# The conditioning of a two-layer diffusion trunk, from row sums on VectorE to matmuls in column groups of TensorE

## The chip, the core and the metric

The kernel runs on one core of a Trainium2 chip. Four engines compute: TensorE (PE in the profile; PEld is its weight loading), VectorE (DVE), ScalarE (ACT) and GpSimd (POOL). SyncE (SP) issues the transfers. Each engine works through its own instructions in order and waits on semaphores for the others. The metric is the device time of one execution in microseconds.

## What is computed

Two layers of a trunk work on 512 latent tokens and 128 context tokens, 1024 wide. Every sub-layer norms its input, scales and shifts it by a conditioning vector, mixes, norms again, multiplies by a gate and adds the residual. The conditioning is one small product for each layer: two vectors of 1024 (one for latent tokens, one for context tokens) times a matrix of 1024 x 6144, cut in six pieces of 1024.

```python
silu_c = jax.nn.silu(c); silu_ctx = jax.nn.silu(c_ctx)
for l in range(DEPTH):                      # 2 layers
    mp = split_mod(silu_ctx @ w_mod[l] + b_mod[l])          # six pieces of 1024
    ms = split_mod((silu_c @ w_mod[l] + b_mod[l])[:, None, :])
    g = norm_g[l]
    hp = modulate(xp, g[0], mp[0], mp[1])   # rmsnorm(x, g) * (1 + scale) + shift
    hs = modulate(xs, g[0], ms[0], ms[1])
    ...                                     # mixer: attention and convolution, or pooling and Fourier
    xp = gated_residual(xp, yp, g[1], mp[2])                # x + gate * rmsnorm(y, g)
    xs = gated_residual(xs, ys, g[1], ms[2])
    hp = modulate(xp, g[2], mp[3], mp[4]); hs = modulate(xs, g[2], ms[3], ms[4])
    xp = gated_residual(xp, swiglu(hp, ...), g[3], mp[5])
    xs = gated_residual(xs, swiglu(hs, ...), g[3], ms[5])
```

So there are 12 pieces, (layer, i) with i from 0 to 5: i = 0 and 3 are shifts, 1 and 4 scales, 2 and 5 gates. Each piece reads 4 MB of weights.

## The kernel before

All large products are made of three matmuls of rounded operands (helper `mm3`, lines 230 to 232: high x high, high x low, low x high), so a weight tile is cast on ACT (L195, L694) and its rest is subtracted on DVE or POOL (L196, L630). The stages follow each other: the opening (norm of the input, transposes, modulation, the first head's Q, K and V), attention and the convolution units, the output projection (`project`, L510) with the chain of norm, gate and residual for each of five token tiles (`chain`), the feed-forward layer in Strassen's form (`ffn`, `strassen`) and its down projection (`project` again), then the same with the odd mixer. In the stages with a written order (`manual_schedule`) DVE, ACT and PE issue in the order in which the code emits; helpers such as `after(d, f)` and `tick` place small steps between matmuls by an estimated clock.

**Conditioning in the opening.** Pieces (0,0) and (0,1) are needed first. Half of each comes as columns of the product: `mod_mm` (L991) is a matmul with two stationary columns (the two vectors) and 256 moving columns of weights, four for a transfer of 512 KB. The other half comes as row sums on DVE: `dot` (L1018) multiplies a 128 x 1024 tile of transposed weights by a broadcast row and sums, once for each vector. A few products of the second vector go to POOL (`dot_pool`) with the sum on ACT. The string START gives the order of all that, engine by engine.

**The other ten pieces** come as such row sums in later stages: `mod_steps` loads eight tiles of 128 x 1024 for a piece and issues two row sums for each (L315); where `MP` says so the second vector's product is on POOL (L305) and its sum on ACT (L308). The generators are advanced one step at a time: (0,2), (0,4), (0,3) in attention and the convolution units (`steps`; what is left is emitted after the last unit), `M0` in Strassen's part of the feed-forward layer 0, `M1` in its down projection, `M2` in the odd mixer, `M4` in the last down projection. A piece ends with small DVE steps (`mod_finish`), and a gate also with a transpose and a store to DRAM (`mod_gate`), from where `gate_rows` (L354) loads it broadcast into the two buffers `t_g`. In attention those two buffers hold the broadcast rows of the row sums until the last of them is done.

Of the kernel before, what the change touches and what calls it, by code (L numbers as in the profile page):

```python
# [19 lines left out]
D = 1024  # L20
# [25 lines left out]
def plan_of(n_cl):  # L46
# [43 lines left out]
).split()  # L90
START_DVE = [5, 7]
# [11 lines left out]
AE = [2.5, 2.8, 4, 5.2]  # L103
DUP = 6
ADD = [5.3]
AC = [0.7, 1, 1.7, 3.4, 4.6]
M0 = [(0,5),(1,0)]
M1 = [(1,1),(1,2)]
M2 = [(1,4),(1,3)]
M3 = []  # L110
M5 = []
M4 = [(1,5)]
DT = [0,1]
# [8 lines left out]
ODD = 'm0 m0 V0 L2 F2 m0 m0 m0 D0 m0 P3 m0 m0 m0 V1 m0 L6 F6 m0 m0 P2 m0 m0 D1 L1 F1 m0 m0 m0 m0 V2 L7 m0 m0 F7 m0 m0 m0 P1 m0 L0 m0 m0 D2 F0 V3 m0 m0 D3 P0 m0 m0 m0 m0 m0 m0'.split()  # L122
DSL = ([1, 3, 6, 10, 12],[])
# [5 lines left out]
def trunk_kernel(ctx: ExitStack, tc: tile.TileContext, a: dict, o: dict):  # L129
# [53 lines left out]
    subg = const.tile([128, 128], F32)  # L183
    junk_a = const.tile([128, D], BF16)
    junk = {}
    mcol = const.tile([128, 2, 6, 2, 8], F32)
    acol = const.tile([128, 2, 2, 2, 8], F32)
    bcol = const.tile([128, 2, 2, 2, 8], F32)
    grow = dr.tile([2, 2, 16, 128], F32)
    srow = dr.tile([2, D], F32)  # L190
    xd = dr.tile([5, 128, D], F32)

# [71 lines left out]
    def mod_finish(l, i):  # L264
        for v in range(2):
            m = mcol[:, l, i, v]
            s = i // 3
            dve.tensor_tensor(out=m, in0=m, in1=bmod[:, l, i], op=ALU.add)
            if i % 3 == 0:
                dve.tensor_copy(bcol[:, l, s, v], m)  # L270
            elif i % 3 == 1:
                dve.scalar_tensor_tensor(out=acol[:, l, s, v], in0=m, scalar=1.0, in1=ng[:, l, 2 * s],
                                         op0=ALU.add, op1=ALU.mult)
            else:
                dve.tensor_tensor(out=m, in0=m, in1=ng[:, l, 2 * s + 1], op=ALU.mult)

    def mod_gate(l, i):
        if i % 3 == 2:
            s = i // 3
            while not free["tr"]:  # L280
                e = pending.pop(0)
                clock[0] = max(clock[0], e[0])
                e[2]()
            tp = trb()
            pe.transpose(tp[:16, :128], mcol[:, l, i].rearrange("p v k -> p (v k)"), ident)
            gs = junk[1]
            act.activation(out=gs, in_=tp[:16, :128], func=AF.Copy)
            nc.sync.dma_start(out=grow[l, s], in_=gs)

    def mod_steps(l, i, rows, get, share=(), early=lambda: True):  # L290
# [1608 lines left out]
```

## Time and profile before

| | before |
|---|---|
| three runs, us | 1460.73, 1461.1, 1469.1 (median 1461.1) |
| profiled execution, its span | 1460.5 us |
| PE busy | 1358.6 us, 93% of the span |
| PEld busy | 1241.1 us, 85% |
| DVE busy | 1143.7 us, 78% |
| ACT, POOL busy | 670.8 us (46%), 208.5 us (14%) |
| mean granted TensorE clock | 0.978 of 2.4 GHz |
| chain that ended last | PE 58%, DVE 26%, issue 6%, ACT 4%, DMA 4% |
| read from memory | 192 MB, 137 GB/s over the span |

The profiled execution's span is 0.6 us under the median of the runs. Busy time is summed over an engine's instructions; the idle time of an engine matters only where that engine is the one that the others wait for. A mean over the span hides that the stages have different limits, so the stretches below are read one by one.

### The profile page before, as it was taken

Reading aid. Unit: us, or ns where it says so; the run is one execution under the profiler, and the core shown is the slowest. Engines: PE = TensorE matmul, PEld = TensorE weight load, DVE = VectorE, ACT = ScalarE, POOL = GpSimd, SP = SyncE. Lnnn points to the kernel's source line nnn. Section 1 sums busy time; section 2 is a strip of 40 time slices with the busy share of each in tenths; the row PEclk is TensorE's granted clock in tenths of the full one; section 3 lists DMA queues with packets and bytes.
Section 4 is the critical chain, followed back from the end, with each engine's and each line's share of the span. In section 5 each row is a group of like instructions: output and inputs, shape, how many; then the busy total and the mean of one; then the engine's idle time right before and its main releaser. Section 6 shows DMA issues by size and latency. Waiting matters only on the chain.

```text
span 1460.5 us, 20973 instructions
## 1 busy us (share of the span) xinstructions
PE 1358.6 (93%) x7892; PEld 1241.1 (85%) x7892; DVE 1143.7 (78%) x2120; ACT 670.8 (46%) x1298; POOL 208.5 (14%) x109
## 2 busy tenths in 40 slices
PE   8898898978889999999998998898899999999997
PEld 3787788977789999999886788777899999997886
DVE  6767876598989978986989589858977777769475
ACT  6445554333555454544336542335454545443343
POOL 2321101342650000000004022006400000000000
PEclk9899999979989999999999999999999999999999
DMA  9412212265433324326763444623122222266452
GB/s 362 149 48 78 79 46 88 89 219 196 142 106 131 116 87 160 130 88 238 259 209 132 156 164 146 222 93 139 61 87 87 88 87 88 87 231 217 144 209 80
DMA packets 61070, 202.06 MB, mean 138 GB/s; under 512 B 9316, under 2 KB 11300, under 8 KB 60968
## 3 DMA queue, kind: packets, MB, share of 16 engines
q1 hardware_dynamic: 60968, 200.71, 39.1%
q8 instruction: 62, 1.02, 0.3%
q14 instruction: 40, 0.33, 0.1%
HBM read 192.26 MB, written 8.43 MB: 137 GB/s over the span
## 4 chain that ended last, share of the span: by engine, by line
PE 58%; DVE 26%; issue 6%; ACT 4%; DMA 4%; POOL 0%; SPq 0%; DVEq 0%; ACTq 0%
PE t_acc L510 13%; PE t_acc L230 10%; PE t_acc L231 10%; PE t_acc L232 10%; DVE t_sm L243 4%; DVE t_pg L315 4%; PE t_tr L230 4%; PE t_tr L232 4%; PE t_tr L231 4%; DVE t_lo L196 2%; PE t_tr L510 2%; DVE t_x L379 1%; DVE t_pg L375 1%; DMA t_pg<-in_w_mod_dram 1%; DVE t_lo L315 1%
## 5 line engine op out<-in xcount | busy, mean ns | idle before, releaser
L230 PE MATMUL t_acc<-t_q,t_hi 128*128 128x320 f32 (+2 forms) x680 | 218.0, 321 | 5.3 <-DVE t_q L1224 2.1
L232 PE MATMUL t_acc<-t_q,t_lo 128*128 128x320 f32 (+2 forms) x696 | 218.7, 314 | 0.2 <-POOL t_lo L196 0.2
L231 PE MATMUL t_acc<-t_q,t_hi 128*128 128x320 f32 (+2 forms) x680 | 214.2, 315 | 3.1 <-POOL t_q L435 3.1
L510 PE MATMUL t_acc<-t_hi,t_pg 128*128 128x512 f32 x696 | 192.0, 391 | 5.5 <-DVE t_pg L196 4.6
L195 ACT ACTIVATE t_hi<-t_raw 128x1024 fp32r<-128x1024 f32 (+1 forms) x110 | 113.5, 1033 | 144.6 <-PE t_acc L510 61.6
L196 POOL TENSOR_TENSOR t_lo<-t_raw,t_hi 128x1024 fp32r<-128x1024 f32 (+1 forms) x36 | 84.0, 2344 | 609.3 <-DVE t_sm L243 407.0
L510 PEld LDWEIGHTS t_acc<-t_hi,t_pg 128*128 128x128 f32 x696 | 129.6, 188 | 35.4 <-DVE t_pg L196 7.3
L230 PEld LDWEIGHTS t_acc<-t_q,t_hi 128*128 128x128 f32 x680 | 131.7, 194 | 6.8 <-ACT t_x L1235 2.4
L231 PEld LDWEIGHTS t_acc<-t_q,t_hi 128*128 128x128 f32 x680 | 131.6, 194 | 3.8 <-POOL t_q L435 3.6
L232 PEld LDWEIGHTS t_acc<-t_q,t_lo 128*128 128x128 f32 x696 | 134.4, 193 | 0.5 <-POOL t_lo L196 0.5
L196 DVE TENSOR_TENSOR t_lo<-t_raw,t_hi 128x1024 fp32r<-128x1024 f32 (+1 forms) x74 | 92.5, 1249 | 46.7 <-ACT t_hi L195 46.4
L510 PE MATMUL t_acc<-t_hi,t_q 128*128 128x512 f32 x416 | 118.4, 402 | 5.5 <-DVE t_pg L1472 2.9
L694 ACT ACTIVATE t_hi<-t_raw 128x512 fp32r<-128x512 f32 x140 | 87.4, 624 | 78.2 <-DVE t_raw L630 78.2
L630 DVE TENSOR_TENSOR t_raw<-t_raw 128x512 f32<-128x512 f32 x160 | 112.0, 720 | 2.2
L630 DVE TENSOR_TENSOR t_lo<-t_raw,t_lo 128x512 fp32r<-128x512 f32 x140 | 97.2, 695 | 21.0 <-ACT t_lo L694 20.7
L630 DVE TENSOR_TENSOR t_hi<-t_raw,t_hi 128x512 fp32r<-128x512 f32 x140 | 96.2, 698 | 14.4 <-ACT t_hi L694 14.4
L510 PE MATMUL t_acc<-t_lo,t_pg 128*128 128x512 f32 x348 | 107.2, 389 | 0.0
L315 DVE SCALAR_TENSOR_TENSOR t_pg<-t_pg,t_g 128x1024 bf16<-128x1024 f32 x80 | 97.6, 1219 | 7.2 <-DMA t_pg<-in_w_mod_dram 6.4
L510 PEld LDWEIGHTS t_acc<-t_hi,t_q 128*128 128x128 f32 x416 | 79.7, 194 | 23.1 <-issue 3.3
L694 ACT ACTIVATE t_lo<-t_raw 128x512 fp32r<-128x512 f32 x140 | 86.8, 620 | 0.6 <-DVE t_raw L630 0.6
L510 PEld LDWEIGHTS t_acc<-t_lo,t_pg 128*128 128x128 f32 x348 | 65.3, 188 | 13.7
L230 PE MATMUL t_acc<-t_q,t_lo 128*128 128x320 f32 x248 | 76.7, 309 | 0.0
(317 smaller groups left out, 3307.5 us busy)
## 6 DMA issues: line engine op xcount, KB each, us to landing
t_raw<-in_w_down_dram SPq DMA_DIRECT2D x56, 512.0 KB, 3.9
t_raw<-in_w_gate_dram SPq DMA_DIRECT2D x44, 512.0 KB, 4.2
t_raw<-in_w_up_dram SPq DMA_DIRECT2D x44, 512.0 KB, 4.2
t_pg<-in_w_mod_dram SPq DMA_DIRECT2D x40, 512.0 KB, 5.4
t_pg<-in_w_down_dram SPq DMA_DIRECT2D x26, 512.0 KB, 5.1
t_x<-in_w_mod_dram SPq DMA_DIRECT2D x24, 512.0 KB, 3.9
t_q<-in_w_mod_dram SPq DMA_DIRECT2D x16, 512.0 KB, 9.0
t_raw<-in_w_mod_dram SPq DMA_DIRECT2D x16, 512.0 KB, 3.9
```

Source lines behind the costliest of these rows:

```text
L195: act.activation(out=hi, in_=src, func=AF.Copy)
L196: (lo_eng or dve).tensor_tensor(out=lo, in0=src, in1=hi.bitcast(F32), op=ALU.subtract)
L230: pe.matmul(out, lhsT=l[0], rhs=r[0], start=start, stop=False, skip_group_check=more)
L231: pe.matmul(out, lhsT=l[0], rhs=r[1], start=False, stop=False, skip_group_check=more)
L232: pe.matmul(out, lhsT=l[1], rhs=r[0], start=False, stop=stop, skip_group_check=more)
L243: return lambda: dve.scalar_tensor_tensor(out=out, in0=in0, scalar=scalar, in1=in1, op0=op0, op1=ALU.mult)
L315: dve.scalar_tensor_tensor(out=junk[0], in0=raws[ft], scalar=1.0, in1=rows[v], op0=ALU.mult, op1=ALU.mult, accum_out=dst)
L375: dve.tensor_tensor(out=P["y"][:, b * 512:(b + 1) * 512], in0=ps[:, b], in1=g[:, b * 512:(b + 1) * 512], op=ALU.mult)
L379: eng.scalar_tensor_tensor(out=x, in0=P["y"], scalar=rs1, in1=x, op0=ALU.mult, op1=ALU.add)
L510: pe.matmul(ps[t][b] if t in parted else ps[t][:, b], lhsT=L[i][:, cols], rhs=w[j][:, b * 512:(b + 1) * 512], start=first and i + j == 0, ...
L630: eng.tensor_tensor(out=out, in0=in0, in1=in1, op=op)
L694: act.activation(out=t_op[:, 0], in_=A[key], func=AF.Copy)
```

## The change

All conditioning is done as fp32 matmuls on TensorE. `col_groups` issues four matmuls for one tile of 128 input rows: each has 32 stationary columns (two of them are the two vectors for this tile, the other 30 are further columns of the same buffer, whose results nobody reads), takes its own 256 (in the opening 128) moving columns of weights, and is placed in its own quarter of the array's columns and of the output's partitions. A piece is eight such groups, summed in PSUM or, in attention, added up by DVE (`gather`); then a copy, two transposes and `mod_finish`. The row sums on DVE, the products on POOL, the sums on ACT and the broadcast rows are gone. The weights of the ten later pieces are no longer transposed on the host.

```diff
+    def col_groups(out, k, rhs, start, stop):
+        n = out.shape[-1]
+        for j in range(4):
+            pe.matmul(out[32 * j:32 * j + 32], lhsT=csil[:, 2 * k:2 * k + 32], rhs=rhs(j), start=start, stop=stop,
+                      tile_position=(0, 32 * j))
+        spend(4 * n)
...
-                dve.scalar_tensor_tensor(out=junk[0], in0=raws[ft], scalar=1.0, in1=rows[v], op0=ALU.mult,
-                                         op1=ALU.mult, accum_out=dst)
+        load(max(ahead(), 1))
+        P = trb()[:, :256] if hold else None
+        for k in range(8):
+            load(k + 1)
+            if not hold:
+                P = tr_when_free()[:, :256]
+                free["tr"] -= 1
+            raw = raws[k]
+            col_groups(P, k, lambda j: raw[:, j * 256:(j + 1) * 256], k == 0 or not hold, k == 7 or not hold)
+            load(k + 1 + ahead())
+            if not hold:
+                def gather(P=P, k=k):
+                    if k:
+                        dve.tensor_tensor(out=R, in0=P, in1=R, op=ALU.add)
+                    else:
+                        dve.tensor_copy(R, P)
+                    free["tr"] += 1
+                after(0.4, gather)
+            yield
+        if hold:
+            R = get()[:, :256]
+            act.activation(out=R, in_=P, func=AF.Copy)
+            yield
...
+        tp = tr_when_free()
+        for h in range(2):
+            pe.transpose(tp[:, h * 128:(h + 1) * 128], R[:, h * 128:(h + 1) * 128], ident)
+        mod_finish(l, i, tp[:, :256])
...
-M0 = [(0,5),(1,0)]
-M1 = [(1,1),(1,2)]
+M0 = [(0,5),(1,0),(1,1)]
+M1 = [(1,2)]
...
     def mods():
         for i in (2, 4, 3):
-            yield from mod_steps(0, i, rows, lambda: xslot([128, D]), MP, lambda: wide)
+            yield from mod_steps(0, i, lambda: xslot([128, D]), amisc[:, :256], lambda: len(wide))
...
-    def mod_mm(e, q, i, half):
+    def mod_mm(e, q, half):
+        if half == 0:
+            vec[q, "o"] = trb()[:, :128]
+        w = pieces[q, half].rearrange("p (k i f n) -> p k i f n", k=2, i=2, f=2)
+        for k in range(2):
+            col_groups(vec[q, "o"], 2 * half + k, lambda j: w[:, k, j // 2, j % 2], half + k == 0, half + k == 4)
...
-    "T.T1 L.r41 D.sl0 T.mm110 A.Tc1 L.q111 A.m1 D.d05 T.F0 L.w3 A.h1 P.l1 L.w2 D.co5 D.d14 T.mm111 A.m5 "
+    "T.T7 D.Tc7 A.sp0 P.sl0 A.h0 D.l0 D.m1 A.h1 P.l1 L.q22 L.q23 T.mm10 T.mm11 T.F0 T.mm12 T.mm13 A.ro1 A.sp1 "
```

The opening is now four stages q of two feature tiles each: four transfers of 512 KB for a stage, four calls of `mod_mm`, a copy (`ro`), a transpose (`ct`), the coefficients on DVE (`cd`), then modulation (`m`), high part (`h`), low part (`l`) and the Q, K, V matmuls of the two feature tiles (`F`).

PE in the opening, from its first instruction. Before (L953 broadcasts the vectors, L991 is `mod_mm`, L977 transposes the input, L1001 the coefficients, L230 is the first of Q, K, V):

```order
L953 MATMUL t_tr<-t_raw,t_q 128x512 x4
L991 MATMUL t_tr<-t_q,csil 2x256 x8
L977 MATMUL t_acc<-ident,t_x 128x128 x30
L991 MATMUL t_tr<-t_q,csil 2x256 x8
L977 MATMUL t_acc<-ident,t_x 128x128 x5
L1001 MATMUL t_tr<-ident,t_pg 128x2 x4
L991 MATMUL t_tr<-t_q,csil 2x256 x8
L977 MATMUL t_acc<-ident,t_x 128x128 x5
L991 MATMUL t_tr<-t_q,csil 2x256 x4
L230 MATMUL t_acc<-t_hi,t_q 128x384
```

And now (L261 is `col_groups`, L948 the transposes, L970 a stage's coefficients, L222 the first of Q, K, V):

```order
L948 MATMUL t_acc<-ident,t_x 128x128 x15
L261 MATMUL t_tr<-t_q,csil 32x128 x8
L948 MATMUL t_acc<-ident,t_x 128x128 x5
...
L970 MATMUL t_tr<-ident,t_q 128x128
L948 MATMUL t_acc<-ident,t_x 128x128 x5
L261 MATMUL t_tr<-t_q,csil 32x128 x16
L222 MATMUL t_acc<-t_hi,t_q 128x384
```

The broadcasts are gone, and the 32 matmuls of 256 columns have become 128 of 128 columns, eight for each of 16 transfers. The last 16 stand behind the Q, K, V matmuls of the sixth feature tile, and the seventh and eighth behind them.

PE in Strassen's part of the feed-forward layer 0, at the border of two products. Before:

```order
L230 MATMUL t_acc<-t_q,t_hi 128x320
L231 MATMUL t_acc<-t_q,t_hi 128x320
L232 MATMUL t_acc<-t_q,t_hi 128x320
L230 MATMUL t_tr<-t_x,t_lo 128x320
L231 MATMUL t_tr<-t_x,t_lo 128x320
L232 MATMUL t_tr<-t_x,t_lo 128x320
```

And now:

```order
L222 MATMUL t_acc<-t_q,t_hi 128x320
L223 MATMUL t_acc<-t_q,t_hi 128x320
L224 MATMUL t_acc<-t_q,t_hi 128x320
L261 MATMUL t_tr<-t_g,csil 32x256 x4
L222 MATMUL t_tr<-t_x,t_lo 128x320
L223 MATMUL t_tr<-t_x,t_lo 128x320
L224 MATMUL t_tr<-t_x,t_lo 128x320
```

A group of four stands between the products here, and at 23 further such borders of this stage.

DVE at the end of the convolution units and the start of the output projection. Before (L315 is a row sum, L196 the low part of a weight tile, L268 `mod_finish`, L370 the start of the first chain):

```order
L315 SCALAR_TENSOR_TENSOR t_pg,mcol<-t_x,t_g 128x1024 x2
L1464 SCALAR_TENSOR_TENSOR t_pg<-t_pg,cw 128x642 x2
L268 TENSOR_TENSOR mcol<-mcol,bmod 128x8
L272 SCALAR_TENSOR_TENSOR acol<-mcol,ng 128x8
...
L315 SCALAR_TENSOR_TENSOR t_pg,mcol<-t_x,t_g 128x1024 x2
L196 TENSOR_TENSOR t_lo<-t_pg,t_hi 128x1024
L315 SCALAR_TENSOR_TENSOR t_pg,mcol<-t_x,t_g 128x1024 x2
L268 TENSOR_TENSOR mcol<-mcol,bmod 128x8
L270 COPY bcol<-mcol 128x8
```

And now (L319 is `gather`, L1404 a convolution step, L271 `mod_finish`, L188 a low part):

```order
L188 TENSOR_TENSOR t_lo<-t_raw,t_hi 128x1024
L319 TENSOR_TENSOR t_g<-t_tr,t_g 128x256 x3
L1390 MEMSET t_pg 128x1
...
L271 TENSOR_TENSOR mcol<-t_tr,bmod 128x8 x2
L274 COPY bcol<-mcol 128x8 x2
L1404 SCALAR_TENSOR_TENSOR t_pg<-t_pg,cw 128x642 x2
L188 TENSOR_TENSOR t_lo<-t_pg,t_hi 128x1024
```

The long row sums between the low parts are gone, the last piece, (0,3), is finished ahead of the last steps of the convolution units and no longer behind low parts of the output projection's weights, and what DVE still does for a tile of conditioning weights there is one addition of 128 x 256.

## Rows read from the trace of the kernel before

**Rows 1.** Stretches: from:to, length, busy of each engine, PE clock, DMA share, GB/s.
```profile
0.00:66.00 66.00, 54.79 (x240) 35.75 (x240) 45.78 (x82) 36.42 (x58) 18.84 (x13) 0.95 0.71 259
66.00:281.00 215.00, 191.54 (x1256) 182.23 (x1257) 145.93 (x327) 108.43 (x288) 34.45 (x16) 0.98 0.22 72
281.00:360.00 79.00, 67.77 (x339) 59.51 (x338) 72.99 (x119) 28.40 (x44) 29.79 (x11) 0.89 0.59 206
360.00:440.00 80.00, 67.12 (x373) 61.05 (x372) 72.78 (x140) 43.31 (x77) 44.49 (x26) 0.91 0.35 119
440.00:680.00 240.00, 240.00 (x1636) 239.73 (x1636) 214.63 (x383) 117.32 (x235) 0.00 (x0) 1.00 0.35 126
680.00:760.00 80.00, 78.77 (x347) 64.59 (x346) 71.00 (x114) 27.91 (x41) 0.00 (x0) 1.00 0.76 262
...
880.00:940.00 60.00, 53.58 (x314) 49.23 (x312) 57.44 (x107) 16.52 (x34) 10.20 (x4) 0.97 0.50 169
...
1300.00:1461.00 161.00, 150.73 (x666) 124.11 (x664) 102.34 (x178) 61.28 (x93) 0.00 (x0) 0.99 0.50 175
```
**Rows 2.** Row sums by line: duration ns min/median/max, first and last start.
```profile
L315 DVE SCALAR_TENSOR_TENSOR t_pg<-t_pg,t_g x80: 1210/1218/1227, 438.4 to 1344.8; 128x1024 bf16<-128x1024 f32 x80
...
L315 DVE SCALAR_TENSOR_TENSOR t_pg<-t_x,t_g x24: 1206/1219/3418, 279.8 to 348.9; 128x1024 bf16<-128x1024 f32 x24
...
L315 DVE SCALAR_TENSOR_TENSOR t_lo<-t_raw,t_hi x16: 1207/1220/3248, 865.6 to 935.4; 128x1024 bf16<-128x1024 f32 x16
...
L315 DVE SCALAR_TENSOR_TENSOR t_q<-t_x,t_g x12: 1215/1219/2848, 82.6 to 196.4; 128x1024 bf16<-128x1024 f32 x12
```
**Rows 3.** Timeline, PE, opening: start us, us, line, operation, count.
```profile
21.80 3.62 PE L991 MATMUL t_tr<-t_q,csil 128*2 128x256 f32 x16
```
**Rows 4.** Timeline, PE, attention: four transposes between the matmuls of a product.
```profile
71.65 0.60 PE L1247 MATMUL t_tr<-ident,t_q 128*128 128x128 f32 x4
72.01 0.39 PE L230 MATMUL t_acc<-t_q,t_hi 128*128 128x320 f32 x1
72.24 0.30 PE L231 MATMUL t_acc<-t_q,t_hi 128*128 128x320 f32 x1
72.38 0.31 PE L232 MATMUL t_acc<-t_q,t_lo 128*128 128x320 f32 x1
```
**Rows 5.** Stretches of the opening, columns as in rows 1.
```profile
0.00:10.00 10.00, 5.82 (x6) 1.66 (x6) 1.47 (x9) 4.64 (x8) 0.20 (x4) 1.00 0.71 256
10.00:20.00 10.00, 8.94 (x33) 3.80 (x34) 6.45 (x16) 7.35 (x13) 1.83 (x1) 1.00 1.03 412
20.00:30.00 10.00, 10.00 (x59) 5.01 (x57) 9.79 (x15) 5.77 (x10) 3.66 (x2) 1.00 1.01 403
```
**Rows 6.** Timeline, opening: coefficient copy, modulation, low part; last of Q, K, V.
```profile
25.45 0.59 ACT L996 ACTIVATE t_pg<-t_tr 2x512 f32<-2x512 f32 x1 [1.59 <-PE t_tr L991]
25.84 0.80 DVE L1047 TENSOR_SCALAR t_pg<-t_pg,acol,bcol 128x512 f32<-128x512 f32 x2
...
31.32 0.82 DVE L1056 TENSOR_TENSOR t_q<-t_pg,t_q 128x640 fp32r<-128x640 f32 x1
...
51.23 0.33 PE L231 MATMUL t_acc<-t_lo,t_q 128*128 128x384 f32 x1
51.40 0.34 PE L232 MATMUL t_acc<-t_hi,t_q 128*128 128x384 f32 x1
...
65.44 0.34 PE L232 MATMUL t_acc<-t_hi,t_q 128*128 128x384 f32 x1
```
**Rows 7.** Groups of DVE from 281 to 360 and 66 to 281: count, busy, mean ns.
```profile
L315 DVE SCALAR_TENSOR_TENSOR t_pg<-t_x,t_g 128x1024 bf16<-128x1024 f32 x24 | 41.2, 1718 | 0.2
...
L1263 DVE SCALAR_TENSOR_TENSOR t_pg<-t_tr,t_pg 128x256 fp32r<-128x256 f32 x20 | 8.4, 422 | 9.5 <-ACT t_pg L1152 7.2 <-ACT pk L1152 1.5 <-PE t_tr L232 0.8
```
**Rows 8.** Waits from 281 to 360, and the gate's load: queue issues, start us.
```profile
PE t_tr L1394 <- DVE t_x L1381: 7.7, 3, 3.1
...
L354 SPq DMA_DIRECT2D t_g<-grow x2: 327/354/382, 348.9 to 350.6; - x2
```

More of the change, by code (lines that the diff above doesn't have):

```diff
@@ L278, in mod_gate @@
         if i % 3 == 2:
             s = i // 3
[L280 to L284, printed above, removed]
+            tp = tr_when_free()
             pe.transpose(tp[:16, :128], mcol[:, l, i].rearrange("p v k -> p (v k)"), ident)
[L286 to L290, printed above, removed]
+            act.activation(out=gsrow, in_=tp[:16, :128], func=AF.Copy)
@@ L322, in mod_steps @@
+        if hold:
+            R = get()[:, :256]
+            act.activation(out=R, in_=P, func=AF.Copy)
+            yield
+        while not hold and any(e[2].__name__ == "gather" for e in pending):
+            pending.pop(0)[2]()
+        tp = tr_when_free()
+        for h in range(2):
+            pe.transpose(tp[:, h * 128:(h + 1) * 128], R[:, h * 128:(h + 1) * 128], ident)
+        mod_finish(l, i, tp[:, :256])
         for _ in range(GY if i % 3 == 2 else 0):
             yield
-        mod_gate(l, i)
@@ L912, in trunk_kernel @@
     vec = {}
-    rows = [gslot() for _ in range(2)]
-    bc = {}
     sums = [small(3), small(2)]
@@ L917, in trunk_kernel @@
     ps0 = {}
-    both = set(START_DVE)
     def ring_slot(key):
@@ L948, in cs @@
     def cs(e):
-        act.activation(out=csil, in_=csil, func=AF.Silu)
-    def bcast(e, v, j):
-        bc[v, j] = trb()
-        pe.matmul(bc[v, j], lhsT=ones, rhs=c_row[v][:, j * 512:(j + 1) * 512], start=True, stop=True)
-    def silu_row(e, v, j):
-        act.activation(out=rows[v][:, j * 512:(j + 1) * 512], in_=bc[v, j], func=AF.Silu)
+        act.activation(out=csil[:, 0:16], in_=csil[:, 0:16], func=AF.Silu)
     def square(e, t):
@@ L984, in tr0_copy @@
             dve.tensor_copy(T0[k], tp0[k])
-    def mod_mm(e, q, i, half):
-        if (q, "o") not in vec:
-            vec[q, "o"] = trb()
-        for j in range(4):
-            k = 4 * half + j
-            pe.matmul(vec[q, "o"][:2, i * 256:(i + 1) * 256], lhsT=csil[:, k],
-                      rhs=pieces[q, i, half][:, j * 256:(j + 1) * 256], start=k == 0, stop=k == 7)
+    def mod_mm(e, q, half):
[4 more added lines that the diff above has]
+            col_groups(vec[q, "o"], 2 * half + k, lambda j: w[:, k, j // 2, j % 2], half + k == 0, half + k == 4)
     def mod_row(e, q):
-        vec[q, "r"] = page([128, NT])[:2, :512]
-        act.activation(out=vec[q, "r"], in_=vec[q, "o"][:2, :], func=AF.Copy)
+        vec[q, "r"] = sq[:, 4096 + 128 * (q % 2):4224 + 128 * (q % 2)]
+        act.activation(out=vec[q, "r"], in_=vec[q, "o"], func=AF.Copy)
     def mod_tr(e, q):
-        vec[q, "t"] = trb()
-        for j in range(4):
-            pe.transpose(vec[q, "t"][:, 2 * j:2 * j + 2], vec[q, "r"][:, j * 128:(j + 1) * 128], ident[:2, :2])
+        vec[q, "t"] = trb()[:, :128]
+        pe.transpose(vec[q, "t"], vec[q, "r"], ident)
     def mod_cols(e, q):
@@ L1090, in trunk_kernel @@
         args = name[len(op):]
-        if op == "d":
-            op, args = name[:2], name[2:]
         todo[op](e, *(int(v) for v in args))
-    for v in range(2):
-        nc.sync.dma_start(out=srow[v:v + 1], in_=rows[v][0:1])
     start.close()
```

191 lines of the change are left out of this document (53 added, 138 removed), and 13 rows, old and new, of the table START.

## The prediction

> **What bounds the kernel now.** I read the stretches first, since 93% of PE busy is a mean over stages with different limits. In Strassen's part of layer 0 (440 to 680) PE is busy 240.0 of 240 us at full clock, and in the down projection behind it 78.8 of 80 [rows 1]. DVE carries many row sums there (214.6 of 240 us), and still PE does not stop: what leaves DVE in these stretches gives nothing, what is put on PE lengthens them. Elsewhere PE stops. From 0 to 66 it is idle 11.2 us, from 66 to 281 23.5 us, from 281 to 440 11.2 + 12.9 = 24.1 us, from 880 to 940 6.4 us. A granted clock below 1 loses more: 0.89 over 79 us and 0.91 over 80 us are 8.7 + 7.2 = 15.9 us of full-rate time between 281 and 440 [rows 1].
>
> Second, the row sums: 148 of about 1.22 us on DVE (80, 24, 12 and twice 16, of which one row is shown), and single ones take up to 3.4 us [rows 2]. They lie unevenly. From 281 to 360 there are 24 of them with 41.2 us of DVE's 73.0 [rows 7, 1]. Third, the waits: in that stretch PE waits 7.7 us for the last scaling of the attention output on DVE, and the load of the first gates is issued only at 348.9, when the last row sum has released the two buffers that it goes to [rows 8, 2]. So DVE bounds the end of attention, PE the feed-forward layers, and the transfers the opening: 412 and 403 GB/s between 10 and 30 us [rows 5].
>
> **The price of one group of four.** The nearest row is `mod_mm` itself: 16 instructions of 256 columns in 3.62 us, 0.226 us each, two for each fp32 matmul, so 0.45 us for one [rows 3]. It uses 2 of the 128 stationary columns and takes no less for it, so the moving columns set its time. No row shows matmuls in separate quarters of the array. The lower bound is that four run side by side, 0.45 us; the upper one that they run one behind the other, 4 x 0.45 = 1.81 us. I take 0.45, because the four share neither array columns nor output partitions, and because the row's time depends on what streams and not on how much of the array it uses; both ends stay for the range. For leaving the other kind of matmul I add 0.1 us: behind four transposes a product's first matmul holds its successor back 0.23 us (72.01 to 72.24), where the next one takes 0.14 [rows 4]. A group is then 0.55 us, and a piece eight groups and about 0.4 us for its two transposes: 4.8 us of PE.
>
> The Trainium skill, page "TensorEngine Tiling (Array Packing)", section "Key Properties", says that changing the tiling mode, and not just the tile, drains the engine. Rows 4 show 0.1 us at a change of kind, though not of tiling. If a drain were as long as what a matmul's duration exceeds its spacing by, 0.31 - 0.14 us, on both sides of each of 80 groups, that would be 27 us in place of 8 and the sum would be 19 us higher, in the upper part of my range.
>
> **The change, stretch by stretch.**
>
> *Opening, -13 us.* Before, the last Q, K, V matmul of the first head starts at 65.44 and ends at 65.8 [rows 6]. Five input tiles, 16 weight tiles of 524 KB and four Q, K, V tiles of 393 KB are 12.6 MB, as before; at 2.6 MB by 10 us, 4.1 and 4.0 MB in the next two tens and the same rate on [rows 5], they have landed at 35 us. A stage needs, behind its last transfer, a call of `mod_mm` (two groups of 128 columns, half of 0.45 us each), the copy (0.59 at most), a transpose (0.3), four small DVE steps (0.8), the modulation (0.8), the cast (0.7) and the low part (0.82) [rows 6]: 4.5 us. The first stage's weights are there at 16 us, so the first Q, K, V matmuls can start at 21 to 23. Six tiles of 15 matmuls at 0.17 us [rows 6] are 15.6 us, and I give 3 us to waits between stages: the sixth ends at 42. Behind it on PE stand the last 16 small matmuls, whose weights landed at 35; with their chain (5 us) and two more tiles (5.2 us) the end is at 52.5. The broadcasts and row sums are gone; ScalarE keeps its squares and half of the copies. If the sixth tile did not hold the last calls up it would be 47; if PE fell to half clock in the wait, 58.
>
> *66 to 281, -3 us.* Twelve row sums (14.6 us) go, 16 gathers come; an operation of DVE on 128 x 256 out of PSUM takes 0.42 us [rows 7], so 6.7 us. PE's idle time and lost clock are 23.5 + 4 = 28 us. I let a third come back, 9 us, since DVE is only at 146 of 215 and stands in some of these waits, not in all. Pieces (0,2) and (0,4) bring 9.6 us of PE, a third of it into idle time: +6.4. Each group now also takes one of two `t_tr` buffers until its gather; behind it queue Q, K, V and the transposes of the heads. That cover is thin and goes into the range with 5 us.
>
> *281 to 440, -24 us.* DVE's 73.0 us from 281 to 360 become about 33: 41.2 of row sums and 2 of their reads out, 8 x 0.42 in. DVE no longer bounds. The gates of the latent tokens can be loaded well ahead of 348.9, since only one of the two buffers is held by conditioning now. Of 24.1 us idle and 15.9 us of clock, 40 together, I take 65%, 26 us; the rest is the chain's own latency, which stays (next late is the last tile's chain). Piece (0,3) brings 4.8 us, half of it into idle time.
>
> *440 to 680, +14.4 us.* Three pieces, (0,5), (1,0) and now (1,1), on an engine without idle time: 3 x 4.8. *680 to 760, +3.6 us:* one piece less the 1.2 us idle. *880 to 940, +1.4 us:* two pieces (9.6) against 6.4 us idle and 1.8 us of clock, which DVE's relief (32 row sums of 57.4 us busy) gives back. *1300 to 1461, +4 us:* one piece, with the little idle time at its start. DVE's row sums in these stretches are priced at nothing, because PE is busy over them [rows 1].
>
> Sum: -13 - 3 - 24 + 14.4 + 3.6 + 1.4 + 4 = -16 us. The profiled execution has 1460.5 us, 0.6 under the median of the three runs; that gives 1444.5 to 1445 us. I say **1445**.
>
> **The rivals.** *(a) Side by side only in part.* Each fp32 matmul is two instructions on the same quarter, so the second must wait for the first; if PE starts its matmuls strictly in order, the next quarter can only run beside the second half. A group then takes 4 x 0.226 + 0.1 = 1.0 us [rows 3]. Eighty groups are 36 us more, of which some 6 fall into idle time, and the opening's ten calls on the path cost 5: 1480 us. For it speaks that the instructions of rows 3 follow each other in pairs; against it that no row shows what may overlap. This is the one that ends on the other side. Above 0.75 us for a group the sum is no longer below the time before, because some 67 of 80 groups fall on a busy PE. The Trainium skill, page "TensorE: Matmul & The Clock Gate", section "Part 3: Packing small matmuls", reports tiles that start 4 ns apart, and also that matmuls start and end strictly in program order; the first speaks for my price, the second for this rival.
>
> *(b) One behind the other*, the change not doing what it says: 1.9 us a group, 109 us more for 80, some 18 of it into idle time, and 14 us more in the opening: 1550 us. For it: rows 3 have one matmul at a time, and nothing in the trace overlaps two on the array.
>
> *(c) The stalls stay.* Between 66 and 440 PE waits for buffers and for ScalarE in place of DVE; a third of what I counted comes back (12 of 35 us): 1468 us. For it: DVE is at only 146 of 215 us in attention. Against: 41 us of row sums in a stretch of 79.
>
> **Chances and range.** The forecast 0.64, with a range of its own of 1427 to 1466 (opening 47 to 58, tail 18 to 34 us, the buffers, half a drain); (a) 0.14, (b) 0.12, (c) 0.10. Leaving out (b) and the outer edges, **1425 to 1488** holds 8 in 10. A measurement of this kernel tells about 1%, 14.6 us, from no change. The forecast lies under 1446.5 a little more often than over it: 0.37, with 0.01 of the others 0.38 for faster; its upper part and most of (c), 0.34 for the same; (a), (b) and a rest of (c), 0.28 for slower.
>
> **What would show it.** Four instructions of a group, in their timeline, starting within some ns of each other, and a group's length of 0.45, 0.9 or 1.8 us from its first start to the next product's. PE's rows of 440 to 680 stretched by 14 us, not by 25 or 45. The last Q, K, V matmul of the opening near 52. From 281 to 440 no wait of PE for the attention output's scaling, the first gate's load ahead of the projection, clock near 1. I am wrong if a group costs over 0.75 us, if the tail keeps its idle time, or if PE's stalls in attention grow by waits for `t_tr`.

## The result, and the profile after

The changed kernel takes 1511.8 us (median; 1509.3 to 1512.7) against 1462.9 us for the kernel before, run beside it: a ratio of 1.033, with a 95% interval of 1.030 to 1.036. The prediction was 1445 us, in a range of 1425 to 1488. The time fell outside the range, on the other side of the time before. The times of the experiments below are medians of fast runs; one run of the third took 2764.6 us and is left out as slow.

The profiled execution has a span of 1510.9 us (1460.5 before). PE is busy 1407.7 us in place of 1358.6, DVE 936.4 in place of 1143.7. The stretches below answer to [rows 1], with the same bounds and columns.

```profile
0.00:66.00 66.00, 39.63 (x393) 31.78 (x394) 25.74 (x63) 24.40 (x38) 12.31 (x10) 0.91 0.71 256
66.00:281.00 215.00, 197.88 (x1346) 179.76 (x1346) 129.97 (x312) 101.33 (x270) 21.94 (x11) 0.98 0.29 95
281.00:360.00 79.00, 78.98 (x479) 68.27 (x477) 36.38 (x91) 24.47 (x40) 10.76 (x5) 1.00 0.43 148
360.00:440.00 80.00, 67.63 (x386) 61.88 (x387) 69.92 (x137) 43.09 (x75) 41.04 (x25) 0.91 0.31 109
440.00:680.00 240.00, 240.00 (x1702) 226.62 (x1701) 169.29 (x301) 108.77 (x220) 0.00 (x0) 1.00 0.38 132
680.00:760.00 80.00, 75.07 (x397) 59.62 (x396) 33.35 (x49) 27.24 (x41) 0.00 (x0) 0.96 0.56 201
```

DVE is relieved as foretold: 36.4 us from 281 to 360, where it had 73.0 (the prediction said about 33), and PE does not stop there any more. But between 0 and 66 PE works only 39.6 us, at a clock of 0.91. The bounds are fixed times, and the work has moved past them; so the two traces are better laid side by side at the places where the same work begins or ends on PE:

| from ... to | before, us | after, us | difference | predicted |
|---|---|---|---|---|
| start ... last Q, K, V matmul of the first head | 65.8 | 73.2 | +7.4 | -13 |
| ... first matmul of the output projection | 252.8 | 251.2 | -1.6 | |
| ... first Strassen product | 113.6 | 106.2 | -7.4 | -27 with the line above |
| ... first matmul of down projection 0 | 246.8 | 265.4 | +18.6 | +14.4 |
| ... its last | 162.7 | 175.0 | +12.3 | +3.6 |
| ... first of the odd output projection | 104.1 | 113.2 | +9.1 | +1.4 |
| ... its last | 65.6 | 67.7 | +2.1 | 0 |
| ... first matmul of the last down projection | 289.1 | 287.9 | -1.2 | 0 |
| ... its last | 151.9 | 163.1 | +11.2 | +4 |

Every line but one is worse than predicted, and they add up to 50 us. Four readings of the trace explain most of it; the experiments test them.

**A group.** PE's timeline (start us, us, engine, line, operation, count) in Strassen's part of layer 0. L222 to L224 are a product's three matmuls, L261 is the eight instructions of four fp32 matmuls:

```profile
513.14 0.31 PE L223 MATMUL t_acc<-t_q,t_hi 128*128 128x320 f32 x1
513.29 0.31 PE L224 MATMUL t_acc<-t_q,t_hi 128*128 128x320 f32 x1
513.53 0.64 PE L261 MATMUL t_tr<-t_g,csil 128*32 128x256 f32 x8
514.10 0.41 PE L222 MATMUL t_tr<-t_x,t_lo 128*128 128x320 f32 x1
514.35 0.30 PE L223 MATMUL t_tr<-t_x,t_lo 128*128 128x320 f32 x1
514.49 0.31 PE L224 MATMUL t_tr<-t_x,t_lo 128*128 128x320 f32 x1
```

The next product starts 0.57 us behind the group's start, where one fp32 matmul of 256 columns alone took 0.45 [rows 3]. So the four lie side by side, and rivals (a), 0.9 us, and (b), 1.8 us, are out. (In the trace the first four of the eight instructions start 6 to 7 ns apart, and the second four 0.22 us behind them: the two instructions of an fp32 matmul follow each other, the four matmuls do not.) But the group starts 0.24 us behind the matmul ahead of it, in place of the usual 0.147, and the first matmul behind it holds the next one back 0.25. From 513.29 to 514.35 are 1.06 us, where two spacings would be 0.29: a group costs PE 0.77 us, not 0.55.

**The opening.** The waits of PE between 30 and 80 us (engine, tile, line <- what it waited for; us in total, times, longest):

```profile
PE t_acc L222 <- ACT t_hi L1004: 5.3, 1, 5.3
PE t_acc L222 <- ACT t_q L996: 2.7, 2, 2.3
PE t_acc L222 <- DVE t_q L1164: 2.1, 1, 2.1
PE t_tr L970 <- ACT t_q L966: 1.3, 3, 0.5
PE t_acc L223 <- POOL t_lo L1009: 1.2, 1, 1.2
```

The first is the wait for the cast of the third Q, K, V weight tile. ScalarE's timeline shows why it is late; the number in brackets is the idle time ahead of an instruction:

```profile
43.68 0.28 ACT L966 ACTIVATE t_q<-t_tr 128x128 f32<-128x128 f32 x1 [5.20 <-PE t_tr L261]
45.82 0.74 ACT L996 ACTIVATE t_q<-t_pg 128x640 fp32r<-128x640 f32 x1 [1.87 <-DVE t_pg L990]
48.16 0.74 ACT L996 ACTIVATE t_q<-t_pg 128x640 fp32r<-128x640 f32 x1 [1.60 <-DVE t_pg L990]
48.81 1.56 ACT L1004 ACTIVATE t_hi<-t_raw 128x768 fp32r<-128x768 f32 x2
```

The casts (L1004) stand behind the copy of the third stage's sums (L966) and two casts of modulated tokens (L996), and ScalarE is idle 5.20 us ahead of that copy. It waits for PE, on which the last quarter of the third stage's small matmuls stands behind a whole Q, K, V tile; of the fourth stage half does. Behind these waits PE's granted clock is low. The stretches behind the two waits of the opening, and behind the one shown next (columns as in rows 1):

```profile
50.00:58.00 8.00, 6.80 (x48) 5.73 (x48) 1.26 (x1) 2.26 (x3) 6.60 (x3) 0.54 0.49 165
...
65.00:73.00 8.00, 8.00 (x30) 7.54 (x30) 1.40 (x2) 1.54 (x3) 0.00 (x0) 0.63 0.44 164
...
711.00:717.00 6.00, 6.00 (x22) 4.24 (x15) 0.00 (x0) 0.25 (x1) 0.00 (x0) 0.58 0.51 182
```

A granted clock of 0.54 to 0.63 is mostly the lower level, 1.2 GHz, where the engine had worked at 2.4 GHz before it stood (1.00 from 36 to 44.3, ahead of the first wait, and from 690 to 705.7, ahead of the last).

**The first group of a down projection.** PE's only wait between 690 and 760:

```profile
PE t_tr L261 <- DMA t_pg<-in_w_mod_dram: 4.9, 1, 4.9
```

The timeline around it, first the queue's issue, then PE:

```profile
703.54 2.01 SPq L303 DMA_DIRECT2D t_pg<-in_w_mod_dram  x3
...
705.09 0.61 PE L502 MATMUL t_acc<-t_hi,t_pg 128*128 128x512 f32 x2
710.63 1.08 PE L261 MATMUL t_tr<-t_pg,csil 128*32 128x256 f32 x8 [4.93 <-DMA t_pg<-in_w_mod_dram]
```

The weights are ordered at 703.54, PE reaches the group at 705.7 and stands until 710.63. Before, such a transfer took nearly as long (issued at 686.56, its first row sum at 692.89), but it was DVE that waited for it, 2.7 us, while PE went on. The last down projection has the same wait (4.9 us at 1349.5).

**Between 66 and 440** two things were added up in the prediction that exclude each other, as the run with one group per piece shows below.

### The profile page after: what moved, and what is told of

It reads as the page before. It is cut to its first block, busy times and chain, and to the rows that moved or that the text cites. A ratio compares the mean times of both kernels' runs of the same rounds, so it can differ in the third digit from the quotient of the medians.

```text
span 1510.9 us, 22263 instructions
## 1 busy us (share of the span) xinstructions
PE 1407.7 (93%) x8732; PEld 1256.9 (83%) x8732; DVE 936.4 (62%) x1830; ACT 651.7 (43%) x1262; POOL 164.6 (11%) x94
## 4 chain that ended last, share of the span: by engine, by line
PE 77%; DVE 12%; ACT 4%; issue 3%; DMA 2%; POOL 1%; SPq 0%; DVEq 0%; ACTq 0%; POOLq 0%
PE t_acc L502 20%; PE t_acc L222 11%; PE t_acc L224 11%; PE t_acc L223 11%; PE t_tr L222 5%; PE t_tr L224 4%; PE t_tr L223 4%; DVE t_sm L235 4%; PE t_tr L261 3%; PE t_tr L502 2%; DVE t_x L371 1%; PE t_acc L1302 1%; DVE t_pg L367 1%; DMA t_pg<-in_w_mod_dram 1%; DVE t_pg L417 1%
## 5 line engine op out<-in xcount | busy, mean ns | idle before, releaser
L222 PE MATMUL t_acc<-t_q,t_hi 128*128 128x320 f32 (+2 forms) x680 | 217.5, 320 | 5.6 <-DVE t_q L1164 2.1
L224 PE MATMUL t_acc<-t_q,t_lo 128*128 128x320 f32 (+2 forms) x696 | 217.4, 312 | 2.0 <-POOL t_lo L188 2.0
L502 PE MATMUL t_acc<-t_hi,t_pg 128*128 128x512 f32 x696 | 199.0, 397 | 3.2 <-DVE t_pg L188 2.4
L187 ACT ACTIVATE t_hi<-t_raw 128x1024 fp32r<-128x1024 f32 (+1 forms) x110 | 113.5, 1033 | 183.8 <-PE t_acc L502 134.9
L188 DVE TENSOR_TENSOR t_lo<-t_raw,t_hi 128x1024 fp32r<-128x1024 f32 (+1 forms) x74 | 90.9, 1229 | 149.8 <-ACT t_hi L187 147.9
L188 POOL TENSOR_TENSOR t_lo<-t_raw,t_hi 128x1024 fp32r<-128x1024 f32 (+1 forms) x36 | 83.3, 2321 | 755.8 <-DVE t_sm L235 444.1
L222 PEld LDWEIGHTS t_acc<-t_q,t_hi 128*128 128x128 f32 x680 | 130.4, 192 | 12.4 <-issue 4.9
L224 PEld LDWEIGHTS t_acc<-t_q,t_lo 128*128 128x128 f32 x696 | 133.2, 191 | 2.7 <-POOL t_lo L188 2.7
L222 PE MATMUL t_acc<-t_q,t_lo 128*128 128x320 f32 x248 | 76.6, 309 | 0.0
L223 PE MATMUL t_acc<-t_q,t_lo 128*128 128x320 f32 x248 | 76.6, 309 | 0.0
```

The costliest lines, as they stand in the source:

```text
L187: act.activation(out=hi, in_=src, func=AF.Copy)
L188: (lo_eng or dve).tensor_tensor(out=lo, in0=src, in1=hi.bitcast(F32), op=ALU.subtract)
L222: pe.matmul(out, lhsT=l[0], rhs=r[0], start=start, stop=False, skip_group_check=more)
L223: pe.matmul(out, lhsT=l[0], rhs=r[1], start=False, stop=False, skip_group_check=more)
L224: pe.matmul(out, lhsT=l[1], rhs=r[0], start=False, stop=stop, skip_group_check=more)
L502: pe.matmul(ps[t][b] if t in parted else ps[t][:, b], lhsT=L[i][:, cols], rhs=w[j][:, b * 512:(b + 1) * 512], start=first and i + j == 0, ...
```

## The experiments

The runs stand beside the kernel before on the same chip, whose median was 1465.8, 1463.2 and 1462.7 us in the three sets. The changes to code are shown against the kernel that each is made from.

**1. The late casts alone.** From the changed kernel, in the order of the opening:

```
-  D.m2 A.h2 D.l2 D.m3 A.h3 D.l3 L.q30 ...  D.l5 A.sp2 P.sl2 A.sp3 P.sl3 T.F4
+  D.m2 A.h2 D.l2 D.m3 A.sp2 P.sl2 A.h3 D.l3 A.sp3 P.sl3 L.q30 ...  D.l5 T.F4
```

> The changed kernel, with one thing moved in the order of the opening: the casts and low parts of the third and fourth Q, K, V weight tile stand ahead of the copy of the third stage's sums, no longer behind the casts of h4 and h5. In the changed kernel PE waits 5.35 us for such a cast (44.34 to 49.69) and 1.20 us for its low part, and then works at half clock; ScalarE was idle between 38.5 and 43.7. If the late casts are the cause, PE then waits only for the third stage's chain, the opening ends at 68 to 70 us in place of 73.2, and the time is about 1507 us in place of 1511.8. If the opening is held by the transfers or by the chain of small matmuls behind the weights, it ends at 72 to 73 and the time is 1511.

Measured: 1510.1 us (ratio 1.030, 1.027 to 1.033); the opening ends at 71.4. PE's waits between 30 and 73:

```profile
PE t_acc L222 <- ACT t_q L996: 7.0, 3, 4.3
PE t_tr L970 <- ACT t_q L966: 1.3, 3, 0.5
PE t_acc L224 <- DVE t_q L999: 0.5, 2, 0.2
```

My theory fell in this form. The wait for the cast is gone, but 7.0 us of waits for the modulated tokens (L996) stand in its place: the casts and the chains of the third and fourth stage were late together. The rival is not confirmed by it either; both leave the order of the small matmuls as it is.

**2. The first group of the down projections two steps later.**

```
     load(max(ahead(), 1))
+    for _ in range(first):
+        yield
...
-        yield from mod_steps(l, i, get, None, lambda: ahead)
+        yield from mod_steps(l, i, get, None, lambda: ahead, 2 if get is page_slot else 0)
```

> The changed kernel, with the first group of the piece in each of the two down projections two steps behind the issue of its weights, in place of right behind it. In the changed kernel PE waits 4.93 us (705.7 to 710.6) and 4.91 us (1349.5 to 1354.4) for these weights, at half clock for some us behind each. If PE stands because the group is the next instruction in its order, both waits go, with the cold clock some 5 to 7 us each: 1498 to 1502 us. If the transfer is late whatever stands behind it, or the products behind the group would have waited for their own weights, the waits only move: 1511.

Measured: 1496.8 us (1.021, 1.019 to 1.024), 15 us less. PE has no wait left in either place, and from 680 to 760 it is busy without a break, at full clock:

```profile
680.00:760.00 80.00, 80.00 (x429) 64.19 (x428) 36.13 (x52) 30.14 (x45) 0.00 (x0) 1.00 0.60 211
```

Down projection 0 falls from 175.0 to 167.0 us, the last from 163.1 to 156.6. Each wait of 4.9 us cost 6.5 to 8.0 with the half clock behind it.

**3. Groups in pairs.**

```
             after(0.4, gather)
+        if pair and k % 2 == 0:
+            continue
+        if pair:
+            yield
         yield
...
-         dots_of(M0, gslot, 1), lambda: (dots_of(M1, page_slot), iter(())))
+         dots_of(M0, gslot, 2), lambda: (dots_of(M1, page_slot), iter(())))
```

> The changed kernel, with the 24 groups of the feed-forward part of layer 0 in pairs: two groups directly behind each other at every second step, so 12 changes into the quartered form and 12 back, in place of 24 and 24. A group there costs 0.77 us of PE from the trace of the changed kernel, of which about 0.43 are its streaming. If the other 0.34 us belong to the two changes of form, 12 pairs save 12 x 0.34 = 4 us: a pair takes about 1.2 us and the time is 1508 us. If the 0.34 us belong to each group (its own weights or its start), a pair takes 1.54 us and the time stays at 1512.

The last line orders a second weight tile ahead, so that a pair has both. Measured: 1507.0 us (1.028, 1.026 to 1.031). The time alone would be weak evidence for 5 us; the timeline is not:

```profile
517.95 0.31 PE L224 MATMUL t_acc<-t_q,t_lo 128*128 128x320 f32 x1
518.19 1.07 PE L261 MATMUL t_tr<-t_g,csil 128*32 128x256 f32 x16
519.19 0.42 PE L222 MATMUL t_acc<-t_x,t_hi 128*128 128x320 f32 x1
519.44 0.31 PE L223 MATMUL t_acc<-t_pg,t_hi 128*128 128x320 f32 x1
```

From 517.95 to 519.44 are 1.49 us; less two spacings of 0.147, the pair costs 1.20 us, and the second group 1.20 - 0.77 = 0.43. So 0.43 us is the streaming of a group, that of one fp32 matmul alone, and 0.77 - 0.43 = 0.34 us belong to the two changes of form; the whole part, from the first Strassen product to the down projection, takes 261.7 us in place of 265.4. The Trainium skill, page "TensorEngine Tiling (Array Packing)", section "Key Properties", says that a change of tiling mode drains the engine; the gaps ahead of the group and behind it are in keeping with that. They do not show that the tiling is the cause, for `mod_mm` has nearly the same price without column groups. In the kernel before, one call of it stands between matmuls of the Q, K, V product:

```profile
37.12 0.34 PE L232 MATMUL t_acc<-t_hi,t_q 128*128 128x384 f32 x1
37.39 1.89 PE L991 MATMUL t_tr<-t_q,csil 128*2 128x256 f32 x8
39.21 0.45 PE L230 MATMUL t_acc<-t_hi,t_q 128*128 128x384 f32 x1
39.49 0.34 PE L231 MATMUL t_acc<-t_lo,t_q 128*128 128x384 f32 x1
```

From 37.12 to 39.49 are 2.37 us; less two spacings of 0.174 and eight instructions, which start 0.216 us apart, 0.30 us are left. What the change consists of, the quarters, the few stationary columns or the fp32 operands, no run here separates.

**4. Column groups in the attention alone.** From the kernel before: `mod_steps` of the changed kernel for the pieces (0,2), (0,4) and (0,3), with their weights laid out for it and the changed kernel's places for these steps; all else as before.

```
-    yield from mod_steps(0, i, rows, lambda: xslot([128, D]), MP, lambda: wide)
+    yield from mod_steps_pe(0, i, lambda: xslot([128, D]), amisc[:, :256], lambda: len(wide))
```

> The kernel before, with only the three conditioning pieces of the attention (scale of the attention norm's gate and both of the feed-forward norm's, 24 groups) taken as fp32 matmuls in four column groups; the opening and all other pieces stay row sums on VectorE. If the stages add up as the two traces say (66 to the first output projection -1.6, from there to the first Strassen product -8.6), it takes 1453 us against 1463. If my prediction of these stages was right in itself and something behind the opening spoilt it, 27 us go: 1436. If the gain between 66 and 440 came from elsewhere (the opening's other order, say), it stays at 1463.

Measured: 1453.8 us, faster than before (0.991, 0.989 to 0.994). From the opening to the output projection it takes 251.3 us (251.2 in the changed kernel, 252.8 before), from there to down projection 0 352.4 (360.4 before). So the gain of this part is real and independent of the opening, and it is the 9 to 10 us that the two traces give, not 27. (The -8.6 us of the expectation end at a wait in the units ahead of the first Strassen product; up to the product itself they are -7.4.)

**5. The attention with one group per piece.** From the kernel of run 4; 21 of the 24 groups and their gathers are left out, so the coefficients are no longer whole:

```
         load(k + 1)
+        if k:
+            load(k + 1 + ahead())
+            yield
+            continue
```

> The kernel with the attention's three pieces on the array, with the first of the eight groups of each piece alone (the other 21 groups and their 21 gathers are left out, the weights are still loaded), to size what these groups cost there. My prediction let half to two thirds of them fall on a busy PE; in PE's rows each holds the products back by 0.77 us. If they cost in full, 21 x 0.77 = 16 us come off 1453.8: 1438. If, as I predicted, a third to a half lies in idle time, 8 to 11 us come off: 1443 to 1446. If PE is not what bounds there, nothing: 1453.

Measured: 1436.5 us (0.981, 0.979 to 0.984), 17.3 us less than run 4 for 21 groups. In the two traces the way from the end of the opening to the first Strassen product is 16.1 us shorter, 0.77 for each group. The stretch from the opening to the output projection, first of run 4 and then of this run (columns as in rows 1):

```profile
64.00:316.00 252.00, 234.77 (x1643) 212.39 (x1642) 149.51 (x366) 114.23 (x294) 28.28 (x14) 0.99 0.35 117
```

```profile
65.00:300.00 235.00, 219.59 (x1474) 208.92 (x1473) 145.90 (x345) 113.55 (x294) 29.54 (x14) 0.99 0.38 126
```

PE's idle time is 17.2 us in the one and 15.4 us in the other: the groups fill none of it. They cost 16 to 17 us of time, although PE has 17 us to spare. It is idle while it waits for a value, and a group stands at its own place in the order, not in that gap. (The gathers went with the groups; PE's busy time alone falls by 15.2 us.)

**6. The opening in another order.** From the changed kernel, the same instructions:

```
-  ... T.mm10 T.mm11 T.F0 T.mm12 T.mm13 A.ro1 A.sp1 P.sl1 T.ct1 T.F1 ... T.mm20 T.mm21 T.F2 ... T.mm22 T.F3 T.mm23
-  A.ro2 T.ct2 ... A.sp2 P.sl2 A.sp3 P.sl3 T.F4 T.mm30 T.mm31 T.F5 T.mm32 T.mm33 A.ro3 T.ct3 ... T.F6 T.F7
+  ... T.mm10 T.mm11 T.mm12 T.mm13 A.ro1 A.h1 P.l1 T.ct1 T.F0 ... T.mm20 T.mm21 T.mm22 T.mm23 A.ro2 T.F1 T.ct2 ...
+  T.mm30 T.mm31 T.mm32 T.mm33 A.ro3 T.F2 T.ct3 ... T.F3 ... T.F4 ... T.F5 ... T.F6 T.F7
```

> The changed kernel, with the same work of the opening in another order: the small matmuls of the second stage stand ahead of the first Q, K, V tile, those of the third behind the first tile, those of the fourth behind the second, each stage's copy and transpose right behind them, and the casts of the Q, K, V weights ahead of the modulations that follow. In the changed kernel PE waits 5.35, 1.20 and 2.33 us for the third and fourth stage's chains and lies at half clock behind, and moving the two casts alone took only 1.8 us off the end of the opening (71.4), because the chains then ended last. If the order is the cause, all chains run beside Q, K, V tiles, the opening ends at 53 to 56 us and the time is 1492. If the transfers, which go on until 33.7 us, and the number of instructions are the cause, it ends near 70 and the time stays at 1509.

Measured: 1491.5 us (1.018, 1.016 to 1.021), 20.3 us less. The opening ends at 53.6. PE's waits from 20 to 60 us are down to

```profile
PE t_acc L222 <- DVE t_q L1164: 2.1, 1, 2.1
PE t_tr L970 <- ACT t_q L966: 0.4, 1, 0.4
PE t_acc L224 <- DVE t_q L999: 0.2, 1, 0.2
```

of which the first lies behind the opening; the granted clock is 1.00 throughout. The same transfers, which go on until about 34 us, now hold nothing up. The order was the cause.

**7. All three mends in the changed kernel**: the edits of runs 2, 3 and 6 together.

```
-    yield from mod_steps(l, i, get, None, lambda: ahead)
+    yield from mod_steps(l, i, get, None, lambda: ahead, 2 if get is page_slot else 0, get is gslot)
```

> The changed kernel with three mends at once: the opening's new order, the first group of the two down projections two steps behind its load, and the 24 groups of the feed-forward part of layer 0 in pairs. If the three causes are apart, their gains add: 1511.8 - 20 - 15 - 4 = 1473 us, still slower than before, because 56 groups lie on a busy PE in the feed-forward and odd stages at 0.77 us (0.6 in pairs). If the waits only move, it stays over 1490.

Measured: 1474.2 us (1.007, 1.005 to 1.010). Three gains of 20.3, 15.0 and 4.8 us make 40.1, and together they give 37.6: within the spread of these runs, some 4 us, the causes are apart. With these stalls mended, the change as a whole is still slower than the kernel before. What is left are above all the 56 groups in the feed-forward and odd stages: run 9 below has the same opening and attention, row sums in place of these groups, and takes 33 us less.

**8. Column groups only where PE does not bound.** Run 4 with the opening of run 6; the rows of silu(c), which the remaining row sums need, are written to memory from the columns at the end of the opening:

```
+    for v in range(2):
+        nc.sync.dma_start(out=srow[v].rearrange("(k p) -> p k", p=128),
+                          in_=csil[:, 0:16].rearrange("p (k v) -> p v k", v=2)[:, v])
     start.close()
```

> Column groups only where PE stops anyway: the opening in the new order of the run on the opening, and the three pieces of the attention; the feed-forward layers, the odd mixer and the last down projection take their row sums on VectorE as before (with the rows of silu(c) written to memory from the columns). The run with the attention's pieces alone took 1453.8 us with the opening of before (its end at 64.3). If the opening ends at 53 to 56, 9 to 11 us come off: 1443 to 1445. If what the opening gains is lost behind it (the attention then waits for its own transfers), it stays at 1452 to 1454.

Measured: 1449.6 us (0.990, 0.988 to 0.993), only 4 us under run 4. The opening ends at 59.1. PE's longest wait from 20 to 60, and then the queue's issues in the timeline (start us, us):

```profile
PE t_tr L263 <- DMA t_q<-in_w_mod_dram: 3.9, 1, 3.9
```

```profile
28.25 4.15 SPq L1099 DMA_DIRECT2D srow<-csil  x2
32.49 3.66 SPq L1104 DMA_DIRECT2D t_q<-in_rope_dram  x1
...
37.64 7.69 SPq L1111 DMA_DIRECT2D cw<-in_conv_w_dram  x1
```

Neither reading that I had written down had this: the opening itself is late, by the two transfers that the kernel adds. The last weights, issued ahead of the two small transfers, come late, and the issues behind them take up to 7.7 us.

**9. The same with these two transfers behind the attention**: the three lines of run 8 are moved.

```
     flush()
     att.close()
+    for v in range(2):
+        nc.sync.dma_start(out=srow[v] ...
```

> The run with column groups in the opening and the attention only, with one thing moved: the two transfers that write the rows of silu(c) to memory stand behind the attention, no longer at the end of the opening. In that run PE waited 3.89 us (37.23 to 41.11) for the last weights of the opening, which had landed by 34 us in the kernels without these transfers, the queue's issues of the next transfers took up to 7.7 us, and the opening ended at 59.1 in place of 53.6. If the many small pieces of these two transfers hold up the weights, the opening ends at 53.6 and the time is 1449.6 - 5.5 = 1444 us. If something else of that kernel is late there, it stays at 1449.

Measured: **1441.2 us** (0.985, 0.983 to 0.988), the fastest version here. The opening ends at 53.9, and the 3.9 us wait is gone. The two transfers carry 8 KB in pieces of 4 bytes. The Trainium skill, page "DMA: Bandwidth & Descriptors", section "Rules for kernel authors", says that a transfer whose last dimension is not contiguous becomes one descriptor for each element. The trace agrees: the packets under 512 bytes in the first 50 us, 5336 in run 8 and 3364 in run 9, differ by nearly the 2048 elements.

**10. Pairs in the attention too**, each pair summed in one PSUM tile. From run 9:

```
-    col_groups(P, k, ..., k == 0 or not hold, k == 7 or not hold)
+    col_groups(P, k, ..., k % 2 == 0, k % 2 == 1)
+    if k % 2 == 0:
+        continue
```

> The same with the attention's 24 groups in pairs, each pair summed in one PSUM tile: 12 changes of form less each way and 12 gathers less on VectorE. At 0.34 us for the two changes, as the pairs of the feed-forward part showed, 12 x 0.34 = 4 us come off what the later writing of the rows gives: 1440 us. If a pair has to wait for the second of its two weight tiles, PE stands in the attention and it is no faster than 1444.

Measured: 1446.7 us (0.988, 0.986 to 0.990), 5.5 us over run 9. The rival was right that PE stands; PE's largest sum of waits from 54 to 320 is

```profile
PE t_tr L263 <- DMA t_x<-in_w_mod_dram: 8.3, 3, 3.8
```

The second weight tile of three pairs had not landed. From the opening to the output projection the trace has 255.2 us where run 9 has 252.6: these waits take more than the fewer changes of form save. Most of the rest lies in the odd mixer and its projection, where both kernels have the same code (172.1 us against 165.2; the other four kernels with this code lie between), so the 5.5 us are not the pairs' price.

## Why the prediction was wrong, by its steps

**What bounds the kernel: right.** PE is busy 240.0 of 240 us from 440 to 680 before and after, and what was put there lengthened it. DVE's relief at the end of attention came as computed, the gate's loads are not held back (the second is issued at 318.9, ahead of the projection, where it was 350.6 [rows 8]), and the wait for the attention output's scaling is gone. What took the place of these waits, by PE's waits from 66 to 320 of the changed kernel, is less:

```profile
PE t_tr L261 <- DVE t_q L188: 3.3, 2, 1.7
...
PE t_tr L261 <- issue: 1.9, 1, 1.9
PE t_tr L222 <- DVE t_g L319: 1.7, 1, 1.7
```

The last is a wait for a gather to give a `t_tr` buffer back, which the prediction had named as the thin cover. From 360 to 440, though, nothing came back: PE is idle 12.4 us there, where it had 12.9, and the clock is 0.91 as before, not near 1.

**The price of a group: streaming right, change of form too small.** 0.43 us against 0.45 is right, and against rivals (a) and (b). The other 0.1 us was 0.34. The step that failed took four transposes between matmuls [rows 4] as the nearest row, and misread it: the matmul ahead of them starts at 71.50, and from there to 72.24 are two spacings of 0.145 and four transposes at 0.11 each, so they cost next to nothing beyond their own time. The nearer row was `mod_mm` between Q, K, V matmuls, shown with run 3, with 0.30 us. The prediction also put beside rows 4 what the Trainium skill says of the drain (page "TensorEngine Tiling (Array Packing)", section "Key Properties") and, from 0.31 - 0.14 us on both sides, 0.34 us, as measured. I put that in the upper part of the range instead of in the sum, where it would have made 1464. For the 64 groups that stand alone 0.22 more are 14.1 us. The 16 of the odd mixer stand in 11 visits and cost 16 x 0.43 + 11 x 0.34 = 10.6 us in place of 8.8. Together that is 16 us. The prediction's own point of decision was 0.75 us, and the price came out at 0.77.

**The opening: the arithmetic right, its reading of the order wrong, 20 us.** The steps gave 52.5, and the reordered kernel ends at 53.6. But the step "I give 3 us to waits between stages" was a choice and not read from the order, which puts the third stage's last matmuls behind a Q, K, V tile and the casts behind that stage's copy. The prediction followed PE's row alone. It had 58 us as its worst case, "if PE fell to half clock in the wait"; the waits (5.35, 1.20 and 2.33 us) were longer than allowed for, and half clock lay behind both of the long ones.

**66 to 440: idle time spent twice, 18 us.** The prediction let 9 + 26 = 35 us of stops come back, and then let a third to a half of 24 groups fall into idle time. From before to run 5, which keeps three groups, 25.6 us go up to down projection 0; with these three groups and the transposes taken off, some 29 come back. That is not far from 35, though in part by luck, for the places were others: 18.3 of the 25.6 us lie ahead of the output projection and 8.1 in it, and from its last matmul to the first Strassen product nothing came back (41.9 us before, 42.7 in the changed kernel and in run 5). The term that failed is the cost: 6.4 + 2.4 = 8.8 us were put down for the groups, and 24 x 0.77 = 18.5 were paid, with some 0.7 for the transposes. Time that is to come back can't also hide work. Rival (c) is half right: less came back than thought, but the stalls at the end of attention did not stay.

**440 to 680: a mis-sized price.** +18.6 in place of +14.4; 24 x 0.77 are 18.5. A pair of transposes costs only 0.23 us here (492.84 to 493.36, less two spacings), not 0.4.

**Both down projections: a wait that I did not look for, 15 us.** The step "one piece less the 1.2 us idle" counted the instructions of the piece and not the DMA in front of it. The rule that a wait moves with the work was at hand: the first row sum of such a piece waited too, on an engine that had slack. Run 2 takes it away, and what is left is +4.3 (predicted 3.6) and +4.7 (predicted 4). That these are near is partly luck: eight groups at 0.77 are 6.2 us, and more idle time came back than was counted.

**The odd mixer: +9.1 in place of +1.4.** Its groups cost 10.6 us. The six kernels here that keep row sums there, with the same code, take 100.5 to 105.1 us for this stage (104.1 before, 100.5 in run 9), the six with groups 112.5 to 113.5. The means differ by 10.1 us: next to nothing came back, and not 8.2. What the stage's idle time waits for was not taken apart.

**The whole.** The order of the opening is 20 us of the 67 us between -16 and +50, the two loads 15, the price of the changes of form 16. The remaining 16 are idle time that was counted as cover or was to come back, mostly from 66 to 440; of these only the attention's part was shown by a run. The +2.1 us of the odd output projection are no effect of the change: five other kernels with the same groups take 64.1 to 66.1 us for it, and those with row sums 64.6 to 69.6.

## What to carry to other kernels

Moving work from a busy engine to another pays where the first one holds the second up, and is paid in full where the second has no gap; in the attention here its gaps were no cover, since the moved instruction did not stand in them. Here 24 of 80 groups and the opening were worth moving, and the best kernel (1441 us) leaves the others on VectorE. With each instruction its waits move too: before it is put on the engine that bounds, its inputs must be on their way early enough, as two steps of lead showed (15 us). And a change of form on the array is a cost per visit (0.34 us here), so a visit should hold as much as its inputs allow, as runs 3 and 10 showed from both sides.

## What the runs showed of the hardware

Four fp32 matmuls of 256 columns in four column groups of 32 stream together in 0.43 us, where one fp32 matmul alone takes 0.43 (two instructions 0.216 apart); entering and leaving this form between full-array matmuls costs 0.34 us more. Eight instructions of fp32 matmuls with two stationary columns and no column groups cost 0.30 us beyond their streaming at such a place. A wait of 4.9 us for a transfer was followed by 6 us at a granted clock of 0.58, and cost 6.5 to 8.0 us in all. Two transfers of 4 KB each, in pieces of 4 bytes, made weights that were issued ahead of them late by 3.9 us of PE's time and the opening 5 us longer (59.1 us in run 8, 53.9 in run 9).
